# Reordering the side engines of a two-layer encoder trunk: queues planned by a timeline model, weights split block by block, small factors on GpSimd

## The chip, the cores and the metric

The kernel runs on one core of a Trainium2 chip. The metric is the time of one execution in device microseconds (us), less being better. TensorE multiplies matrices; VectorE (DVE), ScalarE (ACT) and GpSimd (POOL) prepare its operands and carry its results away; SyncE (SP) issues the transfers from and to the chip's main memory.

## What is computed

The reference is a two-layer trunk over 512 tokens of 1024 features in float32. Layer 0 mixes tokens by differential attention (6 heads, each the difference of two softmaxes over 64 features), layer 1 by chunked gated linear attention (4 heads). Each layer also attends, with 4 heads, to 256 memory tokens, and ends in a gated MLP with a causal convolution of width 3.

```python
def reference(x, mem, ...):
    ...
    for i in range(DEPTH):               # x: (1, 512, 1024)
        h = rms_norm(x, attn_norm[i])
        z = h @ w_in[i]                  # queries, keys, values, gates, memory queries
        o = diff_attention(...) if i % 2 == 0 else gla_attention(...)
        m = memory_cross_attention(...)  # normed queries and keys, 256 memory tokens
        x = x + concat([o, m]) @ w_out[i]
        x = x + conv_ffn(rms_norm(x, ffn_norm[i]), w_up[i], conv_w[i], conv_b[i], w_down[i])
    return x

def rms_norm(x, g):
    y = xf * lax.rsqrt(jnp.mean(xf * xf, axis=-1, keepdims=True) + EPS)
    return y * g
```

(The loop is shortened to its structure.) Queries, keys and the heads' outputs are normed group by group with `rms_norm`, so many small reciprocal square roots are needed.

## The kernel before

**Products.** Float32 precision is reached with three fast matmuls for each product: an operand is split into a high part (rounded) and a low part (the rest), and high x high, high x low and low x high are added up in PSUM. Weights come from memory as `raw` tiles of 128x1024. `split_weights` makes `whi` from one on ScalarE (L202, a copy that rounds) and `wlo` on VectorE (L203, `raw` less `whi`). Each kind has `WB` = 5 buffers, so a copy into a buffer waits until TensorE has read the weights that were there. Activations are split the same way (`xsh` by ScalarE, L235; `xsl` by VectorE, L236).

**Weights.** `make_piece` loads and splits all blocks of the next planned weight (a piece); `weights(key)` makes pieces until the one after that asked for is made too. `gemm` asks at its first unit of work.

**Norms.** `group_norm` squares on ScalarE (L305), sums on VectorE (L306), calls `rsqrt` for one factor per group and multiplies with it on VectorE (L309). `rsqrt` takes Ln and Exp on ScalarE (L192, L193) and one Newton step on VectorE (L178 to L180); in layer 1 (`on_dve`) a shift, a multiplication and three Newton steps, all on VectorE. `token_rsqrt` does the same for a whole token, with the sum taken by a matmul with ones (L343).

**Layer 0's attention.** A loop over t = 0 to 27 interleaves the steps of 24 softmaxes (6 heads x 4 blocks of 128 queries): `logits(t)` (matmuls L619, then a maximum, L624, and the exponentials, L627), `turn(t - 1)` (transposes and copies, L644), `values(t - 2)` (L655), `finish` of a head (transposes of its output into `mix`, split by L235 and L236), `prepare` of the next head (L595) and, from t = `M0` on, `ma.slot` of the memory attention: logits L502, row maximum `nmm` L505 on VectorE, exponentials L509 on ScalarE, transposes and copies L519, values L531. Between them `F.fill(f)` takes further units of projections from a queue until f us of TensorE work are given; `FILL` lists f by stage. `F.flush()` empties it. `ma.queries` (L493 copies) and `keys0` / `keys1` prepare the memory attention.

**Layer 1.** `gla_layer` projects, evacuates at L755, takes the gates' exponentials and logarithms (L813 to L848) and then loads another ScalarE table before the memory attention starts.

**Order.** TensorE's instructions stand in the order in which the program writes them (`manual_schedule`). The queues of ScalarE, VectorE and SyncE are put in order by the framework, which moves instructions as far as their data and buffers allow. Every engine works through its queue in order, so an instruction that waits holds up all that stands behind it.

The function `newton` and the ones around it, as the diff touches them:

Of the kernel before, what the change touches and what calls it, by code (L numbers as in the profile page):

```python
# [32 lines left out]
WB = 5  # L33
STEPS, FILL = (8, 13, 20), (3.2, 2.1, 1.5, 1.3)
K8 = tuple(range(KT))
# [95 lines left out]
def trunk(ctx, tc, head_d, x_t, mem_t, wpack, cols_a_d, cols_d, conv_d, gate_d, rel_bias, diff_lambda, consts, onehot, out):  # L131
# [26 lines left out]
    def blk(b, w=128):  # L158
        return slice(w * b, w * b + w)
# [6 lines left out]
    eps = perm.tile([128, 1], F32, name="eps")  # L166
    V.memset(eps, EPS)

    def transpose(dst, src):
# [6 lines left out]

    def newton(v, y, t):
        V.tensor_mul(t, y, y)  # L178
        V.scalar_tensor_tensor(t, t, -0.5, v, op0=ALU.mult, op1=ALU.mult)
        V.scalar_tensor_tensor(y, t, 1.5, y, op0=ALU.add, op1=ALU.mult)  # L180

    def rsqrt(src, n, inv, on_dve=False, y=None):
        v, t = small("rs_v")[:, :n], small("rs_t")[:, :n]
        y = small("rs_y")[:, :n] if y is None else y
        V.tensor_scalar(v, src, inv, EPS, op0=ALU.mult, op1=ALU.add)
        if on_dve:
            V.tensor_scalar(t.bitcast(I32), v.bitcast(I32), 1, None, op0=ALU.logical_shift_right)
            V.tensor_scalar(y.bitcast(I32), t.bitcast(I32), -1.0, 1597463007.0, op0=ALU.mult, op1=ALU.add)
            newton(v, y, t)
            newton(v, y, t)  # L190
        else:
            A.activation(y, src, AF.Ln, scale=inv, bias=eps)  # L192
            A.activation(y, y, AF.Exp, scale=-0.5)  # L193
        newton(v, y, t)
        return y
# [12 lines left out]
    def load_raw(raw, n):  # L208
        nc.sync.dma_start(raw[:, :n], wpack[at[0], :, :n])
        at[0] += 1  # L210
        return raw

    def make_piece(raws=None):
        parts = []
        for i, (_, _, kk, _, w) in enumerate(blocks[len(made)]):
            n = len(kk)
            raw = load_raw(raw_tile(), n * w) if raws is None else raws[i]
            hi, lo = (wp.tile([128, WTILE], F32R, name=t, tag=t, bufs=WB) for t in ("whi", "wlo"))
            split_weights(slice(0, n * w), raw, hi, lo)
            parts += [(hi[:, blk(j, w)], lo[:, blk(j, w)]) for j in range(n)]  # L220
        made.append(parts)

    used = [0]

    def weights(key):
        i = used[0]
        assert plan[i][0] == key, (plan[i][0], key)
        while len(made) < min(i + 2, len(plan)):
            make_piece()
        used[0] += 1  # L230
        parts, made[i] = made[i], None
        return parts
# [8 lines left out]
    def gemm(sh, sl, nb, key, w, evac, hook=None):  # L241
        got, open_ = [], {}

        def unit(b, k0, k1):
            if not got:
                got.extend(weights(key))
            if k0 == 0:
                open_[b] = bank("mm")[:, :w]
            p = open_[b]
            for k in range(k0, k1):  # L250
                hi, lo = got[k]
                mm(p, sh[k][:, blk(b)], hi, start=k == 0, stop=False)  # L252
                mm(p, sh[k][:, blk(b)], lo, start=False, stop=False)  # L253
                mm(p, sl[k][:, blk(b)], hi, start=False, stop=k == KT - 1)  # L254
            if k1 == KT:
                if hook is not None and b == 0:
                    hook()
                evac(b, open_.pop(b))
        for b in range(nb):
            for k in range(0, KT, 2):  # L260
                F.add(6 * w / 2370.0, lambda b=b, k=k: unit(b, k, k + 2))
# [38 lines left out]

    def group_norm(pool, y, nb, ng, d, on_dve=False):
        ss = small("ss")
        for b in range(0, nb, 2):
            sq = xtile()[:, :2 * ng * d]
            A.activation(sq, y[:, b:b + 2].rearrange("p b n -> p (b n)"), AF.Square)  # L305
            V.reduce_sum(ss[:, b * ng:(b + 2) * ng], sq.rearrange("p (g d) -> p g d", d=d), axis=AX.X)  # L306
        r = rsqrt(ss[:, :nb * ng], nb * ng, 1.0 / d, on_dve)
        yv = y.rearrange("p b (g d) -> p (b g) d", d=d)
        V.tensor_mul(yv, yv, r.unsqueeze(2).to_broadcast([128, nb * ng, d]))  # L309
# [29 lines left out]

    def token_rsqrt(tag, sq, nb, y, on_dve=False):  # L340
        p = bank(tag)
        for b in range(nb):
            mm(p[:, b:b + 1], sq[:, blk(b)], ones[:, 0:1], start=True, stop=True)  # L343
        return rsqrt(p[:, :nb], nb, 1.0 / D, on_dve, y=y)

# [100 lines left out]
    def mem_kv(l):  # L446
        hs, ls = [None] * KT, [None] * KT
        km = [None]

        def operands():  # L450
            if l == 0:
                mem_squares()
            km[0] = xtile().rearrange("p (b n) -> p b n", b=2)
            for k in range(KT):
                if k % 2 == 0:
                    mh, ml = split_tiles()
                c = blk(k % 2, 256)
                hs[k], ls[k] = mh[:, c], ml[:, c]
                split(hs[k], ls[k], memT[k // 2][:, c], c_mem(l, k))

        def ev(b, p):
            A.activation(km[0][:, b], p[:, :256], AF.Copy, scale=r_mem[:, b:b + 1])
            A.activation(vm[l][:, b], p[:, 256:], AF.Copy, scale=r_mem[:, b:b + 1])

        def keys():
            F.need(f"kv{l}")
            p = bank("lg")
            for hp in range(2):
                for b in range(2):
                    transpose(p[:, 256 * hp + 128 * b:256 * hp + 128 * b + 128], km[0][:, b, blk(hp)])  # L470
            A.activation(kmT[l].rearrange("p a b -> p (a b)"), p, AF.Copy, scale=c_mk(l))
        gemm(hs, ls, 2, ("kv", l), 512, ev,
             (lambda: token_rsqrt("lg", mem_acc[0], 2, r_mem)) if l == 0 else None)
        F.add(0.0, lambda: group_norm(None, km[0], 2, 4, 64))
        F.mark(f"kv{l}")
        return operands, keys


    class MemAttn:
        def __init__(self, pool, l, qm, mix, on_dve):  # L480
            self.pool, self.l, self.qm, self.mix, self.on_dve = pool, l, qm, mix, on_dve
            self.live = {}

        def norm(self):
            group_norm(self.pool, self.qm, NB, 4, 64, self.on_dve)

# [73 lines left out]
    def diff_layer(pool, mix, acc):  # L560
# [22 lines left out]
        def norms(pr, i):  # L583
            F.need(f"qk{pr}")
            group_norm(pool, qk[pr][i], NB, 4, 64)

# [16 lines left out]
        def logits(u):  # L603
# [16 lines left out]
            for m in range(2):  # L620
# [9 lines left out]
            V.reciprocal(rc[:, 2 * i:2 * i + 1], s2[:, 1, i:i + 1])  # L630
            V.tensor_scalar(rc[:, 2 * i + 1:2 * i + 2], rc[:, 2 * i:2 * i + 1],
                            s2[:, 0, i:i + 1], nlam, op0=ALU.mult, op1=ALU.mult)
# [14 lines left out]
        def values(u):  # L647
# [8 lines left out]
            if i == 3:  # L656
                rs = small("rs0")
                V.reciprocal(rs[:, :NB], H["s2"][:, 0, :NB])
                o = H["o"] = pool.tile([128, NB, 128], F32, name="o", bufs=2)
                V.tensor_mul(o, po.rearrange("p (b d) -> p b d", d=128),  # L660
                             rs[:, :NB].unsqueeze(2).to_broadcast([128, NB, 128]))
                group_norm(pool, o, NB, 1, 128)

# [20 lines left out]
        prepare(1)  # L684
        ma = MemAttn(pool, 0, qm, mix, False)
        M0 = 8
        for t in range(28):
            if t == 0:
# [6 lines left out]
                ops1, keys1 = mem_kv(1)  # L695
            if t == 5:
                ma.norm()
            if t == 7:
                keys0()
# [13 lines left out]
            f = FILL[bisect(STEPS, t)]  # L713
            if t == 7:
                ma.queries()
# [11 lines left out]
            if t in (7, 8, 15, 16):  # L727
                prepare(2 * (t // 7) + (t + 1) % 8)
            if t == 27:
                F.flush()  # L730
            if t % 4 == 3 and t >= 7:
# [5 lines left out]
    def gla_layer(pool, mix, acc):  # L737
# [11 lines left out]
        def scales():  # L749
            token_rsqrt("sm", acc[0], NB, r_x[:, 2], True)  # L750
            V.tensor_scalar_mul(rq[:, :NB], r, 96.0 ** -0.5)
            V.tensor_scalar_mul(rh[:, :NB], r, 0.5)
# [34 lines left out]

        ma = MemAttn(pool, 1, qm, mix, True)

# [19 lines left out]
        for h in range(4):  # L809
# [8 lines left out]
            V.tensor_tensor_scan(sums[h], keep, la, 0.0, op0=ALU.mult, op1=ALU.add)  # L818
            F.fill(1.5)
        tables("exp_and_others")  # L820
        ma.queries()
        F.fill(2.0)
# [122 lines left out]
        for h in range(4):  # L945
# [15 lines left out]
            outputs(h, 1)  # L961
            group_norm(pool, o_[h], NB, 1, 192, True)
            F.fill(f)
# [31 lines left out]
    def out_proj(l, mix, part, acc, late=None):  # L995
# [13 lines left out]
        units = [(n, i) for n in todo for i in range(len(kk[n // 2]))]  # L1009
        first = [(n, i) for n, i in units if n in todo[:2] and kk[n // 2][i] != late] if late is not None else []  # L1010
        units = first + [u for u in units if u not in first]
# [167 lines left out]
```

## Time and profile before

| what | value |
|---|---|
| median of three runs | 1206.88 us (1206.45 to 1207.43) |
| the profiled execution | 1204.74 us, of which the span is 1202.9 |
| TensorE busy | 1186.2 us (99%), granted clock 1.00 |
| VectorE busy | 761.3 us (63%), 1260 instructions |
| ScalarE busy | 541.6 us (45%), 916 instructions |
| GpSimd busy | 22.7 us (2%), 37 instructions |
| weights split | 214 copies (207.7 us) and 214 low halves (240.0 us) |

Busy time is the sum over an engine's instructions, and the share is that of the span. Matmuls are pipelined: one of 512 columns lasts 0.39 us in the trace, but the next starts 0.227 us after it. The stages in order of time: projections and norms of layer 0 up to 105 us, its attention to 247, the output projection and the scales to 270, the MLP to 630, layer 1's projections to 660, its attention to 815 and the last output projection and MLP to the end.

### The profile page before, as it was taken

What the parts mean: (1) busy time and instruction counts of PE and PEld (TensorE: products, weight loads), DVE (VectorE), ACT (ScalarE), POOL (GpSimd) and SP (SyncE); (2) the same over time, 40 slices, a digit from 0 to 9 for tenths busy, and PEclk for the clock granted to TensorE, in tenths of its full rate; (3) what the DMA queues carried; (4) which work ended last, traced back from release to release, by engine and by line L of the source; (5) the groups of instructions that cost most, each with busy time, mean ns of one, the idle gap of its engine ahead of it and who ended that gap; (6) DMA issues with size and microseconds to landing.
All of it is one profiled execution on the core that took longest, in us unless ns stands there. A gap on an engine that the chain in (4) does not pass through costs nothing.

```text
span 1202.9 us, 14760 instructions
## 1 busy us (share of the span) xinstructions
PE 1186.2 (99%) x5672; PEld 974.0 (81%) x5672; DVE 761.3 (63%) x1260; ACT 541.6 (45%) x916; POOL 22.7 (2%) x37
## 2 busy tenths in 40 slices
PE   9998999999999999999999999999999999999998
PEld 6887787778888888888787888988888888888887
DVE  7566767987776534767547446768777653476741
ACT  6656755554444322434436444536544432243420
POOL 0000000000000000000020000003000000000000
PEclk9999999999999999999999999999999999999999
DMA  8332231232232331322342221143333233232231
GB/s 297 120 95 80 79 103 54 85 116 75 94 116 70 123 105 53 128 82 86 116 139 83 70 70 57 60 130 108 103 98 113 71 123 95 67 126 82 88 114 44
DMA packets 39556, 117.81 MB, mean 98 GB/s; under 512 B 4703, under 2 KB 6040, under 8 KB 39486
## 3 DMA queue, kind: packets, MB, share of 16 engines
q1 hardware_dynamic: 39342, 116.62, 30.1%
q8 instruction: 44, 0.72, 0.2%
q14 instruction: 26, 0.21, 0.1%
q10 hardware_dynamic: 144, 0.26, 0.1%
HBM read 112.65 MB, written 4.21 MB: 97 GB/s over the span
## 4 chain that ended last, share of the span: by engine, by line
PE 92%; DVE 4%; ACT 3%; issue 1%; DMA 1%; DVEq 0%; ACTq 0%
PE ps_mm L270 8%; PE ps_mm L271 8%; PE ps_mm L269 8%; PE ps_sm L270 7%; PE ps_sm L269 7%; PE ps_sm L271 7%; PE ps_mm L252 5%; PE ps_mm L254 5%; PE ps_mm L253 5%; PE ps_tp L269 3%; PE ps_tp L270 3%; PE ps_tp L271 3%; PE ps_lg L270 3%; PE ps_lg L271 3%; PE ps_lg L269 3%; PE ps_tp L171 2%
## 5 line engine op out<-in xcount | busy, mean ns | idle before, releaser
L202 ACT CAST whi<-raw 128x1024 fp32r<-128x1024 f32 (+2 forms) x214 | 207.7, 976 | 246.6 <-PE ps_tp L270 133.8
L203 DVE TENSOR_TENSOR wlo<-raw,whi 128x1024 fp32r<-128x1024 f32 (+2 forms) x214 | 240.0, 1132 | 106.8 <-ACT whi L202 106.0
L269 PE MATMUL ps_mm<-xsh,whi 128*128 128x512 f32 x452 | 179.5, 397 | 1.5 <-ACT xsh L235 1.5
L270 PE MATMUL ps_mm<-xsl,whi 128*128 128x512 f32 x452 | 176.5, 391 | 0.8 <-DVE xsl L236 0.8
L271 PE MATMUL ps_mm<-xsh,wlo 128*128 128x512 f32 x452 | 176.3, 390 | 0.0
L270 PE MATMUL ps_sm<-xsl,whi 128*128 128x512 f32 x380 | 147.9, 389 | 0.0
L271 PE MATMUL ps_sm<-xsh,wlo 128*128 128x512 f32 x380 | 147.9, 389 | 0.0
L269 PE MATMUL ps_sm<-xsh,whi 128*128 128x512 f32 x380 | 147.9, 389 | 0.0
L252 PE MATMUL ps_mm<-whi,xsh 128*128 128x512 f32 (+2 forms) x352 | 138.4, 393 | 0.0
L254 PE MATMUL ps_mm<-whi,xsl 128*128 128x512 f32 (+2 forms) x352 | 131.4, 373 | 0.3 <-DVE xsl L236 0.3
L253 PE MATMUL ps_mm<-wlo,xsh 128*128 128x512 f32 (+2 forms) x352 | 130.7, 371 | 0.0
L1039 ACT ACTIVATE cvo<-u,cv 128x512 f32<-128x512 f32 x88 | 71.5, 814 | 114.0 <-DVE u L1037 113.7
L269 PEld LDWEIGHTS ps_mm<-xsh,whi 128*128 128x128 f32 x452 | 84.9, 188 | 20.0 <-ACT xsh L235 2.2
L270 PEld LDWEIGHTS ps_mm<-xsl,whi 128*128 128x128 f32 x452 | 85.0, 188 | 19.0 <-DVE xsl L236 1.8
L271 PEld LDWEIGHTS ps_mm<-xsh,wlo 128*128 128x128 f32 x452 | 84.9, 188 | 17.7
L1040 DVE SCALAR_TENSOR_TENSOR cvo<-u,cv,cvo 128x512 f32<-128x512 f32 x88 | 65.9, 749 | 31.6 <-ACT cvo L1039 31.4
L269 PEld LDWEIGHTS ps_sm<-xsh,whi 128*128 128x128 f32 x380 | 71.3, 188 | 14.9
L270 PEld LDWEIGHTS ps_sm<-xsl,whi 128*128 128x128 f32 x380 | 71.3, 188 | 14.8
L271 PEld LDWEIGHTS ps_sm<-xsh,wlo 128*128 128x128 f32 x380 | 71.3, 188 | 14.7
L254 PEld LDWEIGHTS ps_mm<-whi,xsl 128*128 128x128 f32 x352 | 66.2, 188 | 12.6 <-DVE xsl L236 0.5
L252 PEld LDWEIGHTS ps_mm<-whi,xsh 128*128 128x128 f32 x352 | 66.4, 189 | 11.0 <-issue 0.9
L253 PEld LDWEIGHTS ps_mm<-wlo,xsh 128*128 128x128 f32 x352 | 66.5, 189 | 9.4
(256 smaller groups left out, 1765.3 us busy)
## 6 DMA issues: line engine op xcount, KB each, us to landing
raw<-in_wpack_dram SPq DMA_DIRECT2D x176, 512.0 KB, 3.5
raw<-in_wpack_dram SPq DMA_DIRECT2D x27, 256.0 KB, 4.1
xt<-in_x_t_dram SPq DMA_DIRECT2D x15, 256.0 KB, 5.3
xres<-xt SPq DMA_DIRECT2D x8, 256.0 KB, 3.0
xt<-xres SPq DMA_DIRECT2D x8, 256.0 KB, 4.1
out_dram<-xt SPq DMA_DIRECT2D x8, 256.0 KB, 2.0
bt<-bias_d SPq DMA_DIRECT2D x6, 256.0 KB, 3.0
raw<-in_wpack_dram SPq DMA_DIRECT2D x4, 384.0 KB, 3.0
```

The lines of the kernel that those rows point to most:

```text
L171: nc.tensor.transpose(dst, src, ident[:n, :n])
L202: A.copy(hi[:, c], raw[:, c])
L203: V.tensor_sub(lo[:, c], raw[:, c], hi[:, c].bitcast(F32))
L252: mm(p, sh[k][:, blk(b)], hi, start=k == 0, stop=False)
L253: mm(p, sh[k][:, blk(b)], lo, start=False, stop=False)
L254: mm(p, sl[k][:, blk(b)], hi, start=False, stop=k == KT - 1)
L269: mm(p, hi[:, blk(n)], bh, start=i == first, stop=False)
L270: mm(p, hi[:, blk(n)], bl, start=False, stop=False)
L271: mm(p, lo[:, blk(n)], bh, start=False, stop=i == last)
L1039: A.activation(c, u[:, 2:], AF.Identity, scale=cv[l][:, 2, j:j + 1], bias=cv[l][:, 3, j:j + 1])
L1040: V.scalar_tensor_tensor(c, u[:, 1:S + 1], cv[l][:, 1, j:j + 1], c, op0=ALU.mult, op1=ALU.add)
```

## The change

- `newton` takes four plain operations in place of three, on an engine that is passed in; `rsqrt` takes a power (exponent −0.5) and one Newton step on GpSimd for all norms, without Ln, Exp or the shift. The mean's scaling is on GpSimd too, or on VectorE where the sum lies in PSUM (`token_rsqrt`).
- The small factor of the differential softmax (`rc`) goes from VectorE to GpSimd.
- `make_block` splits one block of a weight; `gemm` calls it after each unit that belongs to its last row block, rather than splitting a whole piece at its first unit. `product` still asks for whole pieces.
- The memory attention of layer 0 starts one step later (`M0` 9, its norm at t = 6, keys and queries at t = 8); the last `FILL` is 1.25; the flush at t = 27 is gone; in layer 1 the memory queries come within the gates' loop, ahead of the table load; the last output projection begins with four output tiles instead of two.
- `schedule_with_timeline_sim=True`: ScalarE's, VectorE's and SyncE's queues are put in order by the framework's timeline model.

```diff
-STEPS, FILL = (8, 13, 20), (3.2, 2.1, 1.5, 1.3)
+STEPS, FILL = (8, 13, 20), (3.2, 2.1, 1.5, 1.25)
...
+    half = perm.tile([128, 16], F32, name="half")
+    V.memset(half, -0.5)
...
-    def newton(v, y, t):
-        V.tensor_mul(t, y, y)
-        V.scalar_tensor_tensor(t, t, -0.5, v, op0=ALU.mult, op1=ALU.mult)
-        V.scalar_tensor_tensor(y, t, 1.5, y, op0=ALU.add, op1=ALU.mult)
-
-    def rsqrt(src, n, inv, on_dve=False, y=None):
+    def newton(v, y, t, eng=V):
+        eng.tensor_tensor(t, y, y, op=ALU.mult)
+        eng.tensor_tensor(t, t, v, op=ALU.mult)
+        eng.tensor_scalar(t, t, -0.5, 1.5, op0=ALU.mult, op1=ALU.add)
+        eng.tensor_tensor(y, y, t, op=ALU.mult)
+
+    def rsqrt(src, n, inv, y=None, first=G):
...
-        V.tensor_scalar(v, src, inv, EPS, op0=ALU.mult, op1=ALU.add)
-        if on_dve:
-            V.tensor_scalar(t.bitcast(I32), v.bitcast(I32), 1, None, op0=ALU.logical_shift_right)
-            V.tensor_scalar(y.bitcast(I32), t.bitcast(I32), -1.0, 1597463007.0, op0=ALU.mult, op1=ALU.add)
-            newton(v, y, t)
-            newton(v, y, t)
-        else:
-            A.activation(y, src, AF.Ln, scale=inv, bias=eps)
-            A.activation(y, y, AF.Exp, scale=-0.5)
-        newton(v, y, t)
+        first.tensor_scalar(v, src, inv, EPS, op0=ALU.mult, op1=ALU.add)
+        G.tensor_tensor(y, v, half[:, :n], op=ALU.pow)
+        newton(v, y, t, G)
...
+    making = []
+
+    def make_block(raws=None):
+        if len(made) == len(plan):
+            return
+        todo = blocks[len(made)]
+        i = sum(1 for _ in making)
+        _, _, kk, _, w = todo[i]
+        n = len(kk)
+        raw = load_raw(raw_tile(), n * w) if raws is None else raws[i]
+        hi, lo = (wp.tile([128, WTILE], F32R, name=t, tag=t, bufs=WB) for t in ("whi", "wlo"))
+        split_weights(slice(0, n * w), raw, hi, lo)
+        making.append([(hi[:, blk(j, w)], lo[:, blk(j, w)]) for j in range(n)])
+        if i + 1 == len(todo):
+            made.append([p for b in making for p in b])
+            making.clear()
...
-    def weights(key):
+    def weights(key, ahead=True):
...
-        while len(made) < min(i + 2, len(plan)):
+        while len(made) < min(i + 1 + ahead, len(plan)):
             make_piece()
...
-                got.extend(weights(key))
+                got.extend(weights(key, False))
...
+            if b == nb - 1:
+                make_block()
...
-            V.tensor_scalar(rc[:, 2 * i + 1:2 * i + 2], rc[:, 2 * i:2 * i + 1],
+            G.tensor_scalar(rc[:, 2 * i + 1:2 * i + 2], rc[:, 2 * i:2 * i + 1],
...
-        M0 = 8
+        M0 = 9
...
-            if t == 5:
+            if t == 6:
                 ma.norm()
-            if t == 7:
+            if t == 8:
                 keys0()
...
-            if t == 7:
+            if t == 8:
                 ma.queries()
...
-            if t == 27:
-                F.flush()
...
+            if h == 1:
+                ma.queries()
         tables("exp_and_others")
-        ma.queries()
...
-        first = [(n, i) for n, i in units if n in todo[:2] and kk[n // 2][i] != late] if late is not None else []
+        first = [(n, i) for n, i in units if n in todo[:4] and kk[n // 2][i] != late] if late is not None else []
...
-    with _tile.TileContext(nc) as tc:
+    with _tile.TileContext(nc, schedule_with_timeline_sim=True) as tc:
```

More of the change, by code (lines that the diff above doesn't have):

```diff
@@ L211, in load_raw @@
         return raw
-    def make_piece(raws=None):
[L214 to L221, printed above, removed]
+    making = []
[13 more added lines that the diff above has]
+            making.clear()
+    def make_piece(raws=None):
+        n = len(made)
+        while len(made) == n:
+            make_block(raws)
     used = [0]
-    def weights(key):
+    def weights(key, ahead=True):
         i = used[0]
         assert plan[i][0] == key, (plan[i][0], key)
-        while len(made) < min(i + 2, len(plan)):
+        while len(made) < min(i + 1 + ahead, len(plan)):
             make_piece()
@@ L298, in trunk, with group_norm @@
     c_go = lambda t: col(23 + t)
-    def group_norm(pool, y, nb, ng, d, on_dve=False):
+    def group_norm(y, nb, ng, d):
         ss = small("ss")
@@ L306, in group_norm @@
             V.reduce_sum(ss[:, b * ng:(b + 2) * ng], sq.rearrange("p (g d) -> p g d", d=d), axis=AX.X)
-        r = rsqrt(ss[:, :nb * ng], nb * ng, 1.0 / d, on_dve)
+        r = rsqrt(ss[:, :nb * ng], nb * ng, 1.0 / d)
         yv = y.rearrange("p b (g d) -> p (b g) d", d=d)
@@ L338, in squares, with token_rsqrt @@
         acc[0] = sq
-    def token_rsqrt(tag, sq, nb, y, on_dve=False):
+    def token_rsqrt(tag, sq, nb, y):
         p = bank(tag)
@@ L343, in token_rsqrt @@
             mm(p[:, b:b + 1], sq[:, blk(b)], ones[:, 0:1], start=True, stop=True)
-        return rsqrt(p[:, :nb], nb, 1.0 / D, on_dve, y=y)
+        return rsqrt(p[:, :nb], nb, 1.0 / D, y, V)
     def small_vectors():
@@ L473, in mem_kv @@
              (lambda: token_rsqrt("lg", mem_acc[0], 2, r_mem)) if l == 0 else None)
-        F.add(0.0, lambda: group_norm(None, km[0], 2, 4, 64))
+        F.add(0.0, lambda: group_norm(km[0], 2, 4, 64))
         F.mark(f"kv{l}")
@@ L479, in trunk, with __init__ @@
     class MemAttn:
-        def __init__(self, pool, l, qm, mix, on_dve):
-            self.pool, self.l, self.qm, self.mix, self.on_dve = pool, l, qm, mix, on_dve
+        def __init__(self, l, qm, mix):
+            self.l, self.qm, self.mix = l, qm, mix
             self.live = {}
         def norm(self):
-            group_norm(self.pool, self.qm, NB, 4, 64, self.on_dve)
+            group_norm(self.qm, NB, 4, 64)
         def queries(self):
@@ L584, in norms @@
             F.need(f"qk{pr}")
-            group_norm(pool, qk[pr][i], NB, 4, 64)
+            group_norm(qk[pr][i], NB, 4, 64)
         def prepare(h):
@@ L661, in values @@
                              rs[:, :NB].unsqueeze(2).to_broadcast([128, NB, 128]))
-                group_norm(pool, o, NB, 1, 128)
+                group_norm(o, NB, 1, 128)
         def finish(h):
@@ L684, in diff_layer @@
         prepare(1)
-        ma = MemAttn(pool, 0, qm, mix, False)
-        M0 = 8
+        ma = MemAttn(0, qm, mix)
+        M0 = 9
         for t in range(28):
@@ L749, in scales @@
         def scales():
-            token_rsqrt("sm", acc[0], NB, r_x[:, 2], True)
+            token_rsqrt("sm", acc[0], NB, r_x[:, 2])
             V.tensor_scalar_mul(rq[:, :NB], r, 96.0 ** -0.5)
@@ L786, in gla_layer @@
         F.mark("r1")
-        ma = MemAttn(pool, 1, qm, mix, True)
+        ma = MemAttn(1, qm, mix)
         G.memset(gl3.bitcast(F32), 1.0)
@@ L961, in gla_layer @@
             outputs(h, 1)
-            group_norm(pool, o_[h], NB, 1, 192, True)
+            group_norm(o_[h], NB, 1, 192)
             F.fill(f)
```

## The prediction

> **What bounds the kernel now.** I read the page first, then what TensorE waits for, then the timelines around the longest of those waits. The page's busy shares, its chain and its two largest groups:
>
> ```profile
> PE 1186.2 (99%) x5672; PEld 974.0 (81%) x5672; DVE 761.3 (63%) x1260; ACT 541.6 (45%) x916; POOL 22.7 (2%) x37
> ...
> PE 92%; DVE 4%; ACT 3%; issue 1%; DMA 1%; DVEq 0%; ACTq 0%
> ...
> L202 ACT CAST whi<-raw 128x1024 fp32r<-128x1024 f32 (+2 forms) x214 | 207.7, 976 | 246.6 <-PE ps_tp L270 133.8
> L203 DVE TENSOR_TENSOR wlo<-raw,whi 128x1024 fp32r<-128x1024 f32 (+2 forms) x214 | 240.0, 1132 | 106.8 <-ACT whi L202 106.0
> ```
>
> TensorE is busy for 99% and carries 92% of the chain. The order of both programs shows the same 5344 matmuls, moved against each other only a little, so the change acts through TensorE's waits alone. Those of before, the largest seven:
>
> ```profile
> PE ps_lg L502 <- ACT xt L493: 1.8, 1, 1.8
> PE ps_lg L171 <- DVE rs_t L178: 1.6, 1, 1.6
> PE ps_mm L269 <- ACT xsh L235: 1.5, 2, 0.8
> PE ps_sm L655 <- ACT xt L644: 1.5, 1, 1.5
> ...
> PE ps_sm L531 <- DVE xt L519: 0.8, 1, 0.8
> PE ps_mm L270 <- DVE xsl L236: 0.8, 2, 0.5
> PE ps_tp L171 <- ACT qT L595: 0.8, 2, 0.4
> ```
>
> All rows of that view sum to 12.6 us. Measured instead as the excess of one matmul's start over the usual spacing (0.227 us for 512 columns), they are about 14 us, and that is all that a perfect order could win. The sum goes by these excesses. The profiled execution took 1204.74 us (span 1202.9), 2.14 us under the median of 1206.88; I add the difference of the waits to the median. 0.2%, about what a measurement of this kernel can tell from no change, is 2.4 us.
>
> **The price of a GpSimd step.** 159 instructions go to GpSimd: 20 group norms and three token norms (135), and 24 small factors. Its cheap rows and its only two-input row:
>
> ```profile
> L337 POOL TENSOR_TENSOR xt<-xt 128x512 f32<-128x512 f32 x12 | 18.2, 1519 | 380.0 <-ACT xt L335 378.1 <-issue 1.8
> L612 POOL MEMSET bt<- 64x64 f32 x6 | 0.9, 144 | 185.4 <-DMA bt<-bias_d 115.7 <-DVE xt L633 37.8 <-DMA xt<-in_mem_t_dram 31.8
> L1025 POOL MEMSET u<- 128x2 f32 x8 | 0.4, 100 | 208.1 <-PE ps_tp L171 208.1
> ```
>
> An operation on 128x4 to 128x16 costs between 0.10 and 1.29 us (L337's shortest). I take 0.144 from the 64x64 memset, nearest in size, plus 0.06 from one GpSimd instruction to the next and about 0.1 for meeting VectorE, below: 0.3 us. The power has no row; it gets the same price and the same ends. A chain of six is 1.8 us (0.9 to 8) and a hop of 0.13 into GpSimd. Before, the same factor took ScalarE 0.30 + 0.21 and VectorE four times 0.16, about 1.3 us with its hops. VectorE gets 158 small instructions fewer, some 26 us; of its 761 us nearly all lies beside TensorE, so this is worth nothing except where a wait below names VectorE.
>
> **Start, +1.9.** In the changed ScalarE queue a weight copy (0.94 us to the next start) stands ahead of the first evacuations of queries and keys. Before, it stood behind them:
>
> ```profile
> 28.96 0.48 ACT L571 ACTIVATE qs<-ps_mm,r_x 128x256 f32<-128x256 f32 x1 [0.75 <-DMA raw<-in_wpack_dram]
> ...
> 31.57 0.51 ACT L572 ACTIVATE ks<-ps_sm,r_x 128x256 f32<-128x256 f32 x1
> 31.92 1.09 ACT L202 CAST whi<-raw 128x1024 fp32r<-128x1024 f32 x1
> ```
>
> The copy overwrites a buffer that TensorE's last matmul of the stage before reads until 29.91. So: 29.95 + 0.94, one query evacuation 0.37, one key evacuation 0.47, hop 0.05 = 31.8; TensorE's next matmul needs that bank and started at 29.85 before. Loss 1.9. The two norm chains behind it end near 41 and 42 us at 0.2 to 0.3 an operation; their transposes come at 42.7, covered unless GpSimd is dearer.
>
> **Waits at 96.6, 105.8 and 117.4, −1.4.** Excesses 1.69, 1.81 and 0.5, together 4.0. With the memory queries a step later, the values' copy comes nearly in time (0.8 left, as eight interleaved GpSimd operations precede what it needs); the memory keys' norm leaves 0.5, the query copy 0.45, and the transposes of the head output, now stacked with them, 0.85. Sum 2.6.
>
> **First memory logits near 131, +2.7.** VectorE's low half of a weight (1.13 us), which waits for ScalarE's copy, which waits for TensorE's block before, now stands ahead of the row maximum (L505, now L516). Count from TensorE's last reading of the old weight: copy till 1.1, low half till 2.3, two maxima of 0.65 till 3.6, two exponentials of 0.45 from 2.95 on till 3.9. TensorE wants the bank at 2.6: 1.4 lost. A second weight copy (0.94) then stands between the two pairs of exponentials, and the second bank is free at 5.77 and wanted at 4.13: 1.6 lost. Of these 3.0, 0.3 was there (142.8).
>
> **Next memory logits near 173, +1.5.** From TensorE's last reading again (0): copy 0.05 to 1.1, two evacuations (bank done at 1.36) to 2.2, a half copy 0.6, a square 0.6, a copy 0.3; VectorE's reduction waits for the square at 3.36 and the maxima follow at 4.0 and 4.64; exponentials 4.7 to 5.6 and 5.6 to 6.5. Wanted at 4.9 and 5.85, had at 5.7 and 6.6: 0.8 + 0.7.
>
> **End of layer 0's attention, +0.4.** The weights are now split a block at a time, so twelve matmuls (2.7 us) lie over the splitting of the last head's output; 0.94 + 0.56 of the 247.6 wait go. But VectorE was packed from 249.4 to 269.5: eight additions, eight splits, four low halves, seven sums of squares, 18.9 us start to start. The same list starts 1.2 us later, and its last sums of squares, now behind the last split, hold the scale's matmul: 1.9 comes back.
>
> **Layer 1, −2.1.** The wait at 658.3 (excess 1.95) is the memory queries behind the table load; they are now moved ahead of it. In their place TensorE waits for the query norm: from the last gate evacuation 2.3 us to the last square, reduction 0.6, six GpSimd operations 1.8, multiplication 1.2, 6.1 with hops, against 6.5 of matmuls: 0.1 left. At 674.5 (1.01) low halves still stand ahead of the copy of the transposed weights; by the same counting 0.75 is left.
>
> **Nothing.** The other waits (189.5, 211.5, 225, 577, 630, 816.7, 843) keep their producers and neighbours. The last output projection's fours, the fill of 1.25 and the removed flush change only the order of matmuls whose operands are ready; without that cover each would be worth at most a wait of the size above, 0.5. The small factor (L631, 0.27 on VectorE) becomes 0.3 and two hops; 17 of 24 leave VectorE waiting about 0.3 with splits queued behind it, where TensorE has 1 us or more in hand.
>
> Sum: 1.9 − 1.4 + 2.7 + 1.5 + 0.4 − 2.1 = +3.0, so 1209.9 us.
>
> **Rivals.** First, **a port held against GpSimd (+8, 1215)**. The trace has this:
>
> ```profile
> 827.74 3.69 POOL L337 TENSOR_TENSOR xt<-xt 128x512 f32<-128x512 f32 x2 [1.80 <-issue]
> ...
> 828.47 1.79 DVE L236 SCALAR_TENSOR_TENSOR xsl<-xt,cols,xsh 128x512 fp32r<-128x512 f32 x1
> ```
>
> The split of 0.75 took 1.79 beside GpSimd's addition, and the two additions took 3.69 for 2.58. If a small operation has to sit out the VectorE instruction under way, it loses half of a 1.13 us low half, about 0.5, whenever one runs. In the splitting stages that is 3 us more for each chain of six. Three chains stand close before TensorE (start, 96.6, 105.8) with about 1 us of cover each, and the one at 630.6 with less: four times 2 less some overlap is 5 to 8, on top of +3.0 less what already was put in: 1215, at most 1218. Against it: VectorE runs two-input instructions from SBUF for about a quarter of the span, so the mean is 0.14 rather than 0.5; I put 0.1 into the sum. [...] Chance 0.20.
>
> No row shows what a power costs the first time. [...]
>
> Second, **the copies are in time (−3.1, 1203.8)**: the weights' buffers come free before the stage that I counted from, so that the copies put ahead at the start, 131 and 173 are done when evacuations and maxima come due. The 6.1 us of new waits vanish and the gains at 96 to 117 and 658 stay. It decides at a release about 1.9, 1.5 and 0.8 us earlier than mine. For it: the new order puts copies where their queue would otherwise idle (L202 has 246.6 us of idle time before it, mostly for TensorE). Against it: the waits for the named matmuls are in the program. If the tail also keeps its 1.9, 1201.9. Chance 0.25.
>
> Third, **no difference (1206.9)**: waits made and waits taken are both about 6 us; errors of mine of half of either cancel the rest. Chance 0.15.
>
> **Numbers.** My forecast has 0.40, with its own range 1207.5 to 1213 (an operation at 0.2 or 0.45 us; one site read wrongly by 1.5). The range of all is 1203 to 1217: half of the second rival and some of the first rival's end lie outside. Slower by over 0.2%: 0.31 of the forecast, 0.20, 0.02 of the third = 0.53. Faster: 0.24 and 0.02 = 0.26. Within: 0.21.
>
> **What would show it.** In the profile after, TensorE's waits should name an evacuation near 30, the exponentials near 131 and 173 with a weight copy between them, and no longer L493 near 658; VectorE about 26 us less busy; GpSimd's small rows 0.15 to 0.3 us. Rows above 0.5 beside low halves mean the port. Total waits of 10 us or less mean the second rival and make the forecast wrong; a power of over 1 us makes my price wrong.

## Result and the profile after

The changed kernel takes 1222.88 us (median of 4 runs, 1222.1 to 1224.68) against 1206.66 before: 1.39% slower, ratio 1.0139 (1.0121 to 1.0157). Slower was forecast, but by 3 us and not by 16, and the time lies outside the range given. The profiled execution has a span of 1220.3 us, 17.4 more than before.

The page after, engine shares and the chain:

```profile
PE 1192.5 (98%) x5672; PEld 977.1 (80%) x5672; DVE 737.8 (60%) x1102; ACT 532.3 (44%) x882; POOL 100.5 (8%) x196
...
PE 84%; DVE 6%; POOL 3%; ACT 3%; DMA 2%; issue 1%; SPq 0%; ACTq 0%; DVEq 0%; POOLq 0%
```

VectorE is relieved of 23.5 us as intended, but GpSimd is busy for 100.5 us in place of 22.7 and now stands in the chain. What TensorE waits for, after (line, what released it, total, times, longest):

```profile
PE ps_lg L630 <- ACT xt L520: 3.5, 4, 1.4
PE ps_tp L173 <- DVE ks L320: 3.3, 2, 2.6
PE ps_tp L173 <- DVE qm L320: 2.7, 1, 2.7
PE ps_mm L261 <- ACT ks L583: 2.7, 1, 2.7
```

The first row is the pair of waits for exponentials near 139 and the pair near 182; the fourth is the start. All were in the forecast, the start for another reason, as told further down. The second and third are not: multiplications of keys and memory queries with their norm's factor (L320). Both needed a factor from GpSimd; that of the memory queries, ready at 662.02, then also stood behind another VectorE instruction until 663.33. GpSimd's groups, new ones beside the old addition (L348):

```profile
L189 POOL TENSOR_TENSOR rs_y<-rs_v,half 128x16 f32<-128x16 f32 x8 | 23.2, 2903 | 0.4
L348 POOL TENSOR_TENSOR xt<-xt 128x512 f32<-128x512 f32 x12 | 18.6, 1554 | 380.3 <-ACT xt L346 380.1
L189 POOL TENSOR_TENSOR rs_y<-rs_v,half 128x4 f32<-128x4 f32 x10 | 11.1, 1107 | 0.8
...
L189 POOL TENSOR_TENSOR rs_y<-rs_v,half 128x8 f32<-128x8 f32 x2 | 3.3, 1641 | 0.0
L180 POOL TENSOR_TENSOR rs_t<-rs_y 128x4 f32<-128x4 f32 x10 | 3.1, 315 | 0.7
L183 POOL TENSOR_TENSOR rs_y<-rs_y,rs_t 128x16 f32<-128x16 f32 x8 | 3.0, 372 | 0.4
```

L189 is the power. It takes 0.69 us for 2 columns, 1.03 for 4, 1.64 for 8 and 2.90 for 16: about 0.4 us and 0.157 us for each column. A power of 16 columns (2.90 us) is dearer than an addition of 512 (1.55). The other small operations take 0.19 to 0.42 us on the mean of each group, about as priced. The 23 powers are 40 us.

There is a second thing that the waits do not show. Stretches of TensorE around the longest idle times, in the table of windows (width, busy us and matmuls, granted clock, DMA share, GB/s):

```profile
29.92:33.33 3.41, 0.86 (x4) 1.00 0.90 270
33.33:36.74 3.41, 3.41 (x10) 0.50 0.81 291
36.74:40.15 3.41, 3.41 (x17) 1.00 0.02 7
...
142.56:145.97 3.41, 3.41 (x10) 0.50 0.36 141
...
664.80:668.21 3.41, 3.41 (x13) 0.50 0.00 0
```

Behind the waits at the start, near 139 and near 664, TensorE works for 3.41 us at a granted clock of 0.50, and its matmuls of 512 columns come 0.427 us apart in place of 0.227. Against the usual spacing of each shape the three stretches cost 1.6, 1.7 and 1.6 us. Before, the mean clock is 1.000.

### The profile page after: what moved, and what is told of

Same layout as the page of the kernel before. It is cut to its first block, busy times and chain, and to the rows that moved or that the text cites. A ratio compares the mean times of both kernels' runs of the same rounds, so it can differ in the third digit from the quotient of the medians.

```text
span 1220.3 us, 14761 instructions
## 1 busy us (share of the span) xinstructions
PE 1192.5 (98%) x5672; PEld 977.1 (80%) x5672; DVE 737.8 (60%) x1102; ACT 532.3 (44%) x882; POOL 100.5 (8%) x196
## 4 chain that ended last, share of the span: by engine, by line
PE 84%; DVE 6%; POOL 3%; ACT 3%; DMA 2%; issue 1%; SPq 0%; ACTq 0%; DVEq 0%; POOLq 0%
PE ps_mm L281 8%; PE ps_mm L282 8%; PE ps_mm L280 8%; PE ps_sm L280 7%; PE ps_sm L282 7%; PE ps_sm L281 7%; PE ps_mm L261 5%; PE ps_mm L263 5%; PE ps_mm L262 5%; PE ps_tp L280 3%; PE ps_tp L281 3%; PE ps_tp L282 3%; PE ps_lg L281 3%; PE ps_lg L282 3%; PE ps_lg L280 3%; PE ps_tp L173 2%
## 5 line engine op out<-in xcount | busy, mean ns | idle before, releaser
L280 PEld LDWEIGHTS ps_mm<-xsh,whi 128*128 128x128 f32 x452 | 84.9, 188 | 17.4 <-issue 0.5
```

The costliest lines, as they stand in the source:

```text
L280: mm(p, hi[:, blk(n)], bh, start=i == first, stop=False)
```

## Experiments

Two theories stood at first. P: the power on GpSimd is the larger part of the loss. Q: it is the new order of the queues. Two kernels undo one of them in the changed kernel, two do one of them alone in the kernel before.

**The old norm in the changed kernel.** `rsqrt` and `newton` as before, layer 1 on VectorE:

```diff
-        first.tensor_scalar(v, src, inv, EPS, op0=ALU.mult, op1=ALU.add)
-        G.tensor_tensor(y, v, half[:, :n], op=ALU.pow)
-        newton(v, y, t, G)
+        V.tensor_scalar(v, src, inv, EPS, op0=ALU.mult, op1=ALU.add)
+        if on_dve:
...
+        else:
+            A.activation(y, src, AF.Ln, scale=inv, bias=eps)
+            A.activation(y, y, AF.Exp, scale=-0.5)
+        newton(v, y, t)
```

> The changed kernel with the old reciprocal square root (Ln, Exp and Newton on ScalarE and VectorE, all on VectorE in layer 1), all else as changed. Theory P, the power on GpSimd (1.0 to 2.9 us each) is the larger part of the loss: the waits for the normed keys near 46 and 120 and for the normed memory queries near 664 go, and with two of them the low clock behind them, some 10 us: 1212 to 1214 us. Theory Q, the new order of the queues and not the norm is the larger part: not below 1218 us, the waits for the keys' evacuation near 32 and for the exponentials near 139 unchanged.

1212.02 us (1211.38 to 1212.49), ratio to before 1.0041 (1.0026 to 1.0056): 10.9 us of the 16.2 go. P holds. The waits for exponentials stay (3.4 us in all), and stretches of low clock follow near 134 and 274, so 5 us are left for something else.

**The new norm alone, in the kernel before.** The two functions of the change put into the old program.

> The kernel before with the reciprocal square root on GpSimd alone. Theory P: 1214 to 1218 us, with waits of 1 to 3 us for normed queries, keys or memory keys. Theory Q: at most 1210 us, since the old order has enough work ahead of the norms' readers.

1254.33 us, ratio 1.0393 (1.0377 to 1.0408). Both theories are far too low: the same chain costs 47 us in the old order, three times what the whole change costs. About 14 of the 47 us are matmuls at a clock of 0.50 behind the waits. Where it shows:

```profile
PE ps_sm L651 <- ACT xt L640: 8.3, 2, 7.7
PE ps_mm L265 <- DVE xt L976: 5.9, 2, 4.4
PE ps_tp L173 <- DVE ks L305: 4.8, 1, 4.8
```

TensorE's longest wait names a copy of a transpose (L640) that has nothing to do with a norm. The timelines of VectorE, GpSimd and ScalarE before it (near 112) show why (start, duration, and in brackets the idle time and what ended it):

```profile
103.12 0.15 DVE L188 TENSOR_SCALAR rs_v<-ps_lg 128x2 f32<-128x2 f32 x1
106.31 0.69 DVE L305 TENSOR_TENSOR o<-o,rs_y 128x512 f32<-128x512 f32 x1 [3.05 <-POOL rs_y L183]
```

```profile
103.57 1.01 POOL L189 TENSOR_TENSOR rs_y<-rs_v,half 128x4 f32<-128x4 f32 x1
...
106.52 0.54 POOL L183 TENSOR_TENSOR r_mem<-r_mem,rs_t 128x2 f32<-128x2 f32 x1
```

```profile
107.09 0.47 ACT L458 ACTIVATE xt<-ps_mm,r_mem 128x256 f32<-128x256 f32 x1 [4.49 <-POOL r_mem L183]
...
111.70 0.26 ACT L640 COPY xt<-ps_tp 128x128 f32<-128x128 f32 x1
```

VectorE stands 3.05 us and ScalarE 4.49 us before an instruction that wants a factor, with everything else of their queues behind it; the copy then comes after three weight copies that had piled up.

**The changed kernel without the timeline model.**

```diff
-    with _tile.TileContext(nc, schedule_with_timeline_sim=True) as tc:
+    with _tile.TileContext(nc) as tc:
```

> The changed kernel without the timeline model, so that the framework orders the queues as before. Theory P: the norms' waits stay, at most 4 us better than changed (1219 to 1223 us). Theory Q: the wait near 32 and the two near 139 go, each with the low clock behind it, 8 us or more: at most 1215 us.

1248.9 us, ratio 1.0349 (1.0331 to 1.0366): 26 us slower than the changed kernel. Neither theory had this sign. With the power in the program, the model's order is a gain.

**The timeline model alone**, the same line put into the kernel before.

> The kernel before with the queues ordered by the timeline model alone. Theory P: within 5 us of before (1204 to 1211 us). Theory Q: 1212 us or more, with the first evacuations behind a weight copy again and a low clock after it.

1211.96 us, ratio 1.0041 (1.0026 to 1.0056): 4.7 us above the kernel before taken beside it (1207.27) and 5.3 above 1206.66, between P's range and Q's. The first evacuations are not held up, against Q; the one stretch at a recorded clock of 0.50 is near 663, behind the wait for the memory queries. Its first matmuls, from 5.97 to 10.24, also come 0.427 us apart, with the clock on record at 1.00; before they come 0.23 apart there.

Next, what part of the loss is the power's duration, and what the 5 us are that remain without it.

**A multiplication in place of the power.**

```diff
-    V.memset(half, -0.5)
+    V.memset(half, 0.001)
...
-        G.tensor_tensor(y, v, half[:, :n], op=ALU.pow)
+        G.tensor_tensor(y, v, half[:, :n], op=ALU.mult)
```

> The changed kernel with a multiplication by 0.001 in place of the power, so that its norms are left out of the result; every instruction stays on its engine and in its queue. Theory P1, the power's own duration is the loss that was not foreseen: the chains take 1.5 to 2.5 us and the time is 1211 to 1214 us, the waits for normed keys and memory queries near 46, 120 and 664 under 0.6 us. [...]

1212.66 us (1210.36 to 1214.59), ratio 1.0057 (1.004 to 1.0075). P1: that 23 instructions are powers and not multiplications makes 10.2 of the 16.2 us; the move to GpSimd with its hops is no dearer than the old norm (1212.02). The instructions stay on their engines, as expected, but not all at their places in the queue: for another operation the model makes another order (a weight copy that starts at 30.40 in the changed kernel comes at 33.26 here, behind the first evacuations). So the 10.2 us are the power's duration with the order that the model makes for it. The kernel's waits:

```profile
PE ps_lg L630 <- ACT xt L520: 3.7, 4, 1.6
PE ps_mm L281 <- DVE xsl L245: 2.3, 4, 0.8
PE ps_tp L173 <- DVE xsl L245: 1.8, 2, 1.1
PE ps_mm L261 <- ACT ks L583: 1.6, 1, 1.6
```

Keys (L320) and memory queries are gone from the list, the start is at 1.6 in place of 2.7. This kernel is the one that the forecast had in mind: a chain of six at 0.2 to 0.5 us each.

**The old norm without the model.**

> The changed kernel with the old reciprocal square root and without the timeline model: what is left of the change are the blocks, the steps moved, the queries ahead of the table, the fours and the small factor. Theory R1, the timeline model's order is what costs 5 us once the norm is back: 1203 to 1207 us, without the waits near 30 and 132. Theory R2, the blocks and moved steps cost it: 1210 us or more.

1206.13 us (10 runs), ratio 0.9997 (0.9987 to 1.0007). R1 by its time: the model costs 6 us once the norm is cheap. But the pair of waits near 133 (excess 1.62 and 1.43) stays without the model, so it is not the model's, and one of 0.99 near 31 stays too.

**The old norm with whole pieces**, the model kept:

```diff
-                got.extend(weights(key, False))
+                got.extend(weights(key))
...
-            if b == nb - 1:
-                make_block()
```

> The changed kernel with the old reciprocal square root, weights split by whole pieces again, the timeline model kept. Theory R1: as with blocks, 1210 to 1214 us. Theory R2, the blocks put copies ahead of the exponentials near 132 and 175: these two pairs of waits (2.9 and 1.2 us) go, about 1208 us, and the wait near 248 for the last head's split comes back (1.5 us).

1211.59 us, ratio 1.0044 (1.0029 to 1.0059). The blocks are not the loss (1212.02 with them), against R2; near 133 one wait of 2.4 us and one of 0.5 are left in place of 1.45 and 1.43, near 175 the waits are as they were, and none comes back near 248.

**The memory queries ahead of the table, alone** in the kernel before:

```diff
             F.fill(1.5)
+            if h == 1:
+                ma.queries()
         tables("exp_and_others")
-        ma.queries()
```

> The kernel before with layer 1's memory queries moved ahead of the table load, alone. If the wait of 1.95 us at 658 is the table load's, it goes: 1205 us (1204 to 1206). Rival: the queries then wait for their norm on VectorE instead, no difference beyond 0.5 us.

1204.19 us (10 runs, 1203.05 to 1204.99), ratio 0.9982 (0.9972 to 0.9991). The wait at 658 goes and 0.47 comes for the norm: a real gain of about 2 us (1.1 to 3.4 by the interval).

Last, the rest: whether the order needs the other edits, where the pair near 133 comes from, and what an idle time costs.

**The new norm and the model, the other edits left out.**

> The kernel before with the reciprocal square root on GpSimd and with the timeline model, the other edits left out. Theory S1, the model knows the chain's length and moves other work ahead of the instructions that wait for it, whatever the program around: 1219 to 1226 us, 30 us less than the same norm in the old order. Theory S2, it takes the steps moved by hand (memory attention one step later) to cover the chains: 1235 us or more.

1224.81 us, ratio 1.0155 (1.0138 to 1.0172). S1, by its time. All eight combinations of norm, order and the other edits (us):

| norm, order | the rest as before | the rest as changed |
|---|---|---|
| old, framework's | 1206.7 | 1206.1 |
| old, model's | 1212.0 | 1212.0 |
| on GpSimd, framework's | 1254.3 | 1248.9 |
| on GpSimd, model's | 1224.8 | 1222.9 |

The model takes 30 and 26 us off the long chain and puts 5 to 6 on the short one. The edits by hand gain 0 to 5.

**The small factor on VectorE**, in the changed kernel:

```diff
-            G.tensor_scalar(rc[:, 2 * i + 1:2 * i + 2], rc[:, 2 * i:2 * i + 1],
+            V.tensor_scalar(rc[:, 2 * i + 1:2 * i + 2], rc[:, 2 * i:2 * i + 1],
```

> The changed kernel with the small factor of the softmaxes on VectorE as before. Theory P: the factors stand in GpSimd's queue behind powers of up to 2.9 us, and VectorE waits for them; without them 1 to 3 us less, 1220 to 1222 us. Rival: they always had cover, 1222 to 1224 us, no change.

1224.35 us (1221.67 to 1224.97), ratio to before 1.0145 (1.0129 to 1.016), that is no difference from the changed kernel's 1.0139. The rival holds: VectorE waits for the factor, but TensorE has cover there.

**The steps back.** The changed kernel with the old norm, no model, and:

```diff
-        M0 = 9
+        M0 = 8
...
-            if t == 6:
+            if t == 5:
                 ma.norm()
-            if t == 8:
+            if t == 7:
                 keys0()
...
-            if t == 8:
+            if t == 7:
                 ma.queries()
```

> The changed kernel with the old norm, without the timeline model and with the memory attention's steps where they were (start at 8, norm at 5, keys and queries at 7): blocks, queries ahead of the table, fours and the small factor remain. Theory T1, the moved steps make the pair of waits for exponentials near 133 (1.6 and 1.4 us): it goes, the waits near 97 and 107 (1.7 and 1.8) come back, and what is left of the change's gains (queries 2, the last head's split 2) shows: 1202 to 1205 us. Theory T2, the blocks make that pair of waits: it stays, 1206 to 1209 us.

1202.21 us (1201.06 to 1203.38), ratio 0.9963 (0.995 to 0.9976): the fastest of all, better than both kernels. T1: the pair near 133 is gone and was made by the steps moved. Its waits:

```profile
PE ps_lg L173 <- DVE rs_y L182: 2.6, 1, 2.6
PE ps_mm L270 <- ACT ks L592: 1.6, 1, 1.6
...
PE ps_mm L290 <- DVE xsl L254: 0.8, 3, 0.3
```

The wait for the memory keys' norm is back (2.6, near 106), and a stretch of low clock behind it costs another 1.0 us. The one near 97 is not, and the last head's split (3.25 us of excess from 247 to 269 before) is down to 1.3 (0.38 and two times 0.47).

**What an idle time costs.** In the kernel before, nine times in layer 0's MLP:

```diff
+        def probe(k):
+            p = bank("tp")
+            mm(p[:, :128], ones, ones, start=True, stop=True)
...
+            V.tensor_copy(dl[:, :128], p[:, :128])
+            for _ in range(k):
+                G.memset(dl[:, :], 0.0)
+            if k == 0:
+                G.memset(dl[:, :1], 0.0)
+            p = bank("tp")
+            mm(p[:, :128], ones, dl[:, :128], start=True, stop=True)
...
+                if l == 0 and 1 <= q < 10:
+                    probe(q - 1)
```

> The kernel before with nine artificial waits of TensorE added in layer 0's MLP, where it is otherwise never idle: a matmul, a VectorE copy, 0 to 7 GpSimd memsets of 0.52 us and a matmul that reads the result (added work; the MLP's own results are not touched). Theory C1, a single wait of about 2.5 us or more is followed by a stretch of matmuls at 0.427 us each in place of 0.227, and shorter ones are not: slow stretches of 1 to 2 us lost behind the waits with 3 or more memsets, none behind the others. Theory C2, the slow stretches of the changed kernel have another cause than its idle time: none here, whatever the wait.

The memsets are 0 to 8, one more than the expectation says (and a small one where there is none). The waits came out at 1.1 to 5.6 us in steps of about 0.58 and the kernel at 1256.96 us (one run). Windows behind the first three and the sixth:

```profile
289.00:291.50 2.50, 2.26 (x11) 1.00 0.38 121
313.00:315.50 2.50, 2.32 (x11) 1.00 0.39 108
...
338.50:341.80 3.30, 3.30 (x9) 0.50 0.56 174
...
485.30:492.00 6.70, 6.02 (x15) 0.50 0.21 73
```

Behind 1.08 and 1.57 us the clock stays at 1.00. With 2.15 us and every longer wait it falls to 0.50 for 3.41 us, or twice that with three of the longest four, and the matmuls lose about 1.6 us, or 2.7 to 2.9. C1 holds, with a lower limit than it said.

That limit is not one for a single wait. In each trace the low stretches begin a whole number of times 3.41 us apart (32 and 153 times in the changed kernel; 8, 8, 27, 9, 8, 9 and 40 in the probe), as if the clock were set for one slot of 3.41 us after another. Cut into such slots, the kernel before has its wait of 1.95 us at 658 on both sides of a slot's end, and the kernel with the model alone has one of 1.91 us within a slot. Before:

```profile
654.44:657.85 3.41, 2.29 (x10) 1.00 0.00 0
657.85:661.26 3.41, 2.74 (x15) 1.00 0.02 5
```

The model alone:

```profile
659.14:662.55 3.41, 1.66 (x11) 1.00 0.00 0
662.55:665.97 3.42, 3.42 (x10) 0.50 0.03 5
```

The fourteen traces, from 14 to 1188 us, have 34 such stretches. In the slot before 33 of them TensorE was busy for 1.72 us or less, about half of it; the exception is that near 142 in the changed kernel, behind a slot with 2.15 us. In every slot at full clock that another at full clock followed it was busy for 1.73 us or more. This is read from the traces; no run was made to test it.

## Why the prediction was wrong, point by point

**The step that failed is the price of the power.** It had "the same price and the same ends" as any small operation, 0.3 us, 1.29 at most. It took 0.69 to 2.90. The upper end was the duration of another operation on 512 columns, which says nothing of an operation that is slow for each column. A chain of six on 16 columns took 4.4 us for the memory queries in place of 1.8:

```profile
657.62 0.21 POOL L188 TENSOR_SCALAR rs_v<-ss 128x16 f32<-128x16 f32 x1 [10.14 <-DVE ss L317]
657.92 2.90 POOL L189 TENSOR_TENSOR rs_y<-rs_v,half 128x16 f32<-128x16 f32 x1
660.90 0.21 POOL L180 TENSOR_TENSOR rs_t<-rs_y 128x16 f32<-128x16 f32 x1
661.19 0.22 POOL L181 TENSOR_TENSOR rs_t<-rs_t,rs_v 128x16 f32<-128x16 f32 x1
661.50 0.22 POOL L182 TENSOR_SCALAR rs_t<-rs_t 128x16 f32<-128x16 f32 x1
661.80 0.22 POOL L183 TENSOR_TENSOR rs_y<-rs_y,rs_t 128x16 f32<-128x16 f32 x1
```

Between the traces of the changed kernel and of the kernel with the multiplication lie 11.8 us (the medians are 10.2 apart). They stand at these places: 1.2 at the start, of which the token norm's power is 0.7 and a later first weight copy 0.5; 1.2 near 46, at the normed queries and keys; 2.4 near 120, at normed keys; 2.9 near 664, at the memory queries; −0.3 near 139; 1.1 at small waits between 190 and 645; and 3.2 more of low clock. Sum 11.7.

**The low clock was not in the forecast at all.** It was put at nothing, and it adds 4.9 us in the changed kernel: the waits at the start and near 664 leave TensorE idle for most of a slot (busy for 0.86 and 0.68 us of 3.41), and a third stretch follows the pair near 139. The wait that brings it is not of one length here: 2.15 us sufficed in the probe, and 1.91 in the kernel with the model alone, while 1.95 at 658 before did not.

**With the power taken out, the sum was near, in part by luck**: 1212.7 against 1209.9. Its terms, forecast and measured in that kernel:

| term | forecast | measured |
|---|---|---|
| start | +1.9 | +1.8, but not by the copy |
| 96 to 117 | −1.4 | −2.6 |
| memory logits near 131 | +2.7 | +2.9, and 1.7 of low clock |
| memory logits near 173 | +1.5 | +1.1 |
| end of layer 0's attention | +0.4 | +0.4 |
| the table's wait, 658 | −1.85 | −1.95 |
| transposed weights, 674 | −0.25 | +0.4 |
| "nothing" | 0 | +0.55 near 192, +0.4 near 782, +0.7 near 821, +0.8 near 847 |

The measured terms add up to 6.2 us where 5.6 lie between the spans; differences under 0.3 us each take the rest back. Counting instructions in queue order by the durations of the profile found the terms near 131, 173 and 658 to within 0.4; from 96 to 117 more was gained. Of the waits said to "keep their producers and neighbours", those near 192 and 821 kept the producer and grew, and that near 847, for the low half of an activation, is new.

**The start was right by luck.** The copy that was to hold the first evacuations stands behind them in the kernel with the multiplication, and with the old norm too:

```profile
30.39 0.47 ACT L582 ACTIVATE qs<-ps_mm,r_x 128x256 f32<-128x256 f32 x1 [0.37 <-POOL r_x L183]
...
33.26 1.10 ACT L198 CAST whi<-raw 128x1024 fp32r<-128x1024 f32 x1
```

In the changed kernel it does stand ahead, but it ends at 31.43 and the norm's factor (`r_x`), which the evacuation needs as well, comes at 31.55:

```profile
30.40 1.03 ACT L198 CAST whi<-raw 128x1024 fp32r<-128x1024 f32 x1
31.58 0.47 ACT L582 ACTIVATE qs<-ps_mm,r_x 128x256 f32<-128x256 f32 x1
```

What holds the evacuations is an earlier copy, which starts when its weights have landed: VectorE's low half behind it stands ahead of the norm's first step. From that copy's start to the first evacuation pass 3.66 us before, 3.94 with the multiplication and 4.65 with the power. The copy itself starts at 25.30 in the profile before, at 26.45 and 26.93 in these two. But two more profiles have the old instructions up to there (the queries alone ahead, and the probe), and in them it starts at 26.62 and 26.32, and TensorE waits 1.2 and 0.6 us near 31. So of the 1.43 us by which the first evacuation comes later with the multiplication (30.39 against 28.96), 1.15 are when the weights came, which differs from run to run with the program unchanged.

What stands between near 131 is as foreseen, ScalarE's timeline after:

```profile
138.47 0.47 ACT L520 ACTIVATE xt<-ps_lg,nmm 128x256 f32<-128x256 f32 x1
...
138.92 1.04 ACT L198 CAST whi<-raw 128x1024 fp32r<-128x1024 f32 x1
139.86 0.48 ACT L520 ACTIVATE xt<-ps_lg,nmm 128x256 f32<-128x256 f32 x1
```

The reason was only half right: copies stand there, but whole pieces (with the model) do not remove the wait, and the steps moved back (without it) do.

**First rival, GpSimd held by VectorE.** Wrong as the cause, since 10.2 of the 16.2 us go with the power alone. That a port is what holds was the author's guess, and no run shows one. The hold itself shows in the small operations: one of 0.21 us took 1.11, up to the end of the low half that ran:

```profile
104.56 1.22 DVE L199 TENSOR_TENSOR wlo<-raw,whi 128x1024 fp32r<-128x1024 f32 x1
...
106.20 1.23 DVE L199 TENSOR_TENSOR wlo<-raw,whi 128x1024 fp32r<-128x1024 f32 x1 [0.35 <-ACT whi L198]
```

```profile
104.73 1.11 POOL L188 TENSOR_SCALAR rs_v<-ss 128x16 f32<-128x16 f32 x1
...
106.09 2.90 POOL L189 TENSOR_TENSOR rs_y<-rs_v,half 128x16 f32<-128x16 f32 x1
```

The 112 small operations of the norms take 0.26 us on the mean and 0.20 at the median, so the holds cost about 0.06 each by an estimate from these two, where 0.1 was put into the sum. Behind that 0.1 stood an estimate that VectorE's two-input instructions, and they alone, hold GpSimd for a quarter of the span. No run sets one kind of instruction against another, and the trace before has 552 us of two-input instructions without a PSUM operand, 46% of the span; the low halves of weights alone are 240.0 us, 20%. The second low half started 0.11 us after a power and took its usual 1.23, and the power its usual 2.90: here a power does not keep VectorE out. The other way round it is held: one on 4 columns at 134.94, begun 0.2 us into a low half, took 1.89 us in place of about 1.02. So an operation begun during a low half was held in both cases, and a low half begun during a power was not.

**Second rival, copies in time.** Wrong by its time: all three new waits are there. At the start the copy was indeed in time, and the wait came all the same. **Third, no difference:** right only for the other edits together, with the old norm and the old order (ratio 0.9997). The first power of the run took 1.03 us, the same as a later one on 4 columns (1.03), so nothing was paid there for a first call.

What is not settled is which of the model's assumed durations made its order 5 to 6 us worse for the old norm; the waits differ at many places by about 1 us each.

## What to carry to other kernels

An operation that the trace has never shown has no upper bound from rows of other operations: leave the range open, or measure it alone first, with its growth by columns. Moving a step off a busy engine is no gain when the new engine's latency lands in front of instructions that wait in order; count the chain, then what is queued behind each of its readers. An edit of the program, a costlier step and a new queue order that come together should be split by their combinations: here one hid another's 26 us, and one edit of the lot (queries ahead of the table), or all without norm, model and moved steps, was a gain.

## What the runs showed of the hardware

- GpSimd's power costs 0.69, 1.03, 1.64 and 2.90 us for 2, 4, 8 and 16 columns on 128 partitions; the norms' other operations on these sizes took 0.20 at the median.
- In the probe seven idle times of TensorE, of 2.15 to 5.6 us, each brought 3.41 us, or twice that, at a granted clock of 0.50, a loss of 1.6 to 2.9 us beside the wait; those of 1.08 and 1.57 us did not. In 33 of the 34 cases of all traces TensorE had been busy for 1.72 us or less of the 3.41 us before.
- A low half of a weight on VectorE that began 0.11 us after a power of 16 columns took its usual 1.23 us, and the power its 2.90; a power of 4 columns begun during a low half was held (1.89 us in place of 1.02), as a small operation was (1.11 in place of 0.21).
